# The FFN's down product of a decoder block by one level of Strassen's algorithm, with its input's quarter sums passed through DRAM

## The chip, the cores and the metric

One NeuronCore of a Trainium2 chip runs the whole kernel. The metric is device time in microseconds of one execution; each number quoted for a kernel is the median of its timed runs, and one further execution was recorded by the hardware profiler. All matrix products are made in three passes: an fp32 operand x is split into h (x rounded to the engine's fp32r type) and l = x - h, and x·w is summed as xl·wh + xh·wh + xh·wl. Every product below therefore needs three matmuls where one would stand.

## The reference, cut to what matters

The block is a gated token mixer followed by a SwiGLU FFN, for 512 tokens of width 2048 and a hidden width of 5632:

```python
h2 = rms_norm(x, g_pre_ffn[l]) * (1 + scale_f) + shift_f
f = (jax.nn.silu(h2 @ w_ffn_gate[l]) * (h2 @ w_ffn_up[l])) @ w_ffn_down[l]
x = x + gate_f * rms_norm(f, g_post_ffn[l])
```

The last product, (512 x 5632) @ (5632 x 2048), is the down product. The norm behind it needs the sum of squares of a token's whole row of f, so no output can be finished before all of that token's row is there.

## The kernel before

**The plan.** The kernel is one list `plan` of `Step`s. A step has a source in DRAM (`src`, up to 128x1024 of weights), the matmuls that use it (`mm`), and optional hooks. `run` walks the list and writes the instructions of all engines, each engine then works its own queue in that order. At step i it first emits the `post` hook of step i-1 and the `pre` of step i; then, for the steps up to i+`ahead` (2, or 3 in the Strassen steps), it loads (`fetch`, a DMA on SP's queue into one of the rotating `raw` tiles) and divides (`divide`, line 80's helpers: ACT casts `raw` to `wh`, DVE subtracts to get `wl`); then loads up to i+`far`; then the `late` hook of step i-1; then the matmuls of step i. `fix` is a hook that adds weight tiles together on DVE before they are divided (`prefix`, called two steps further ahead). So what stands in a `post` hook comes on its engine before the split of step i+`ahead`, what stands in a `late` hook comes behind it.

**The up product.** It already goes by one level of Strassen's algorithm (Winograd's form): `strassen(u)` for each of the units 1 to 10 of 512 hidden columns (unit 0 is done plainly by `fill`). Both operands are cut in halves of tokens (HT = 256), inner dimension and columns; seven products of quarter size take the place of eight. Eight pairs of steps (`mm1` for PSUM banks A and B, `mm2` for D and C) are followed by four blocks of three steps (`mm3_` for A, `mm4` for D, `mm5` for C); the sums of weights are made by `fix1` (a 1024-wide and a 512-wide add; the second is also written to DRAM as `t2_d` by POOL's queue) and `fix5`. At the seam between pairs and blocks the hooks `post1`, `late1`, `post2`, `late2` move banks through `u2` and `hn`. The result `hn` (tokens x 512 hidden) of unit u-1 is turned by `hid_out` during unit u: 16 PE transposes into bank B, ACT copies to `hT`, POOL's queue writes four 256 KB tiles `hid_d`.

**The down product.** Two halves g of 1024 output columns, each over 44 steps k of 128 hidden rows. A step loads a 128x1024 weight tile, reads back `hid_d[k]` (POOL's queue, `h_load`), splits both (`divide`, `d_split`), and runs 24 matmuls `d_mm` (four token tiles, two column tiles, three passes) into eight banks. `down_first` starts with half the banks because the last unit's transposes still need the others. In the last four steps of the second half the order is turned to go token tile by token tile, so that `d_evac`, `d_sum` and `d_end` of the tiles 0 to 2 (squares on ACT, scaling, root, four adds with `x1` and the stores) run beside the matmuls of the next tile. `x1` is read back by POOL's queue in the steps 26 to 29 of the second half, four loads of 256 KB each.

Of the kernel before, what the change touches and what calls it, by code (L numbers as in the profile page):

```python
# [15 lines left out]
P = 128  # L16
S = 512
# [16 lines left out]
LAST = 4  # L34
# [40 lines left out]
def body(ctx, tc, nc, a, out):  # L75
# [81 lines left out]
    more = {"F": 1 << 30}  # L157

    def fetch(i):
        o = i - more["F"] - 4  # L160
        if o >= 0 and o % 6 < 3:
# [38 lines left out]
    def divide(i):  # L200
        if i < len(plan) and i not in parts:
            while i not in loaded:
                load(i)
            st, raw = plan[i], loaded[i]
            prefix(i)
            o = i - more["F"] - 2
            p, n = (more["p"], 2) if o >= 0 and o % 5 < 2 else (wp, 3)
            h = p.tile([P, 1024], F32R, name="wh", tag="wh", bufs=n)
# [1104 lines left out]
    hid = {}  # L1313
    hid_d = [drp.tile([P, S], F32, name=f"hid_d{k}") for k in range(KF)]
    t2_d = [[drp.tile([P, 1024], F32, name=f"t2_d{i}{m}") for m in range(4)] for i in range(2)]
# [62 lines left out]

    def hid_out(u, js, bs):

        for j, b in zip(js, bs):
            for t in range(4):
                nc.tensor.transpose(b[:, t * P:(t + 1) * P], hn_of(u, t)[:, j * P:(j + 1) * P], ident)
# [15 lines left out]
    def strassen(u):  # L1399
# [51 lines left out]
        for m in range(4):  # L1451
# [28 lines left out]
            def mm5(h, l, m=m):  # L1480
                for j in range(2):
                    product(B["C"], Xh[:, 1, 8:], Xl[:, 1, 8:], 2 * m + j, h, l, j, False, m == 3 and j == 1)
                if m < 2:
                    hid_out(u - 1, range(2 * m, 2 * m + 2), B["B"])
# [11 lines left out]
            plan.append(Step(src5, mm5, fix=fix5, post=post5 if end else None, late=late5 if end else None, **kw))  # L1496
# [8 lines left out]

    def d_start():
        O["sp"].release()
        xpool.release()
        p = E["p"] = pool("dp")
        E["row"] = p.tile([P, D], F32, name="frow")  # L1510
        gq.dma_start(E["row"], gg_d[16:32].rearrange("a b -> (a b)").partition_broadcast(P))
        E["f"] = p.tile([P, 4, 1024], F32, name="fo")
        E["ssq"] = p.tile([P, 4, 4], F32, name="fssq")
        E["sum"] = p.tile([P, 8], F32, name="fsum")
        E["pad"] = p.tile([P, 104], F32, name="fpad")

    def h_load(k):
        p, tag, n = (E["p"], "hin", 4) if "p" in E else (O["xp"], "hT", 3)
        hid[k] = p.tile([P, S], F32, name=tag, tag=tag, bufs=n)
        gq.dma_start(hid[k], hid_d[k])  # L1520

    def d_split(k):
        p, n = (E["p"], LAST) if "p" in E else (O["xp"], 1)
        hh = p.tile([P, S], F32R, name="hh", tag="hh", bufs=n)
        hl = p.tile([P, S], F32R, name="hl", tag="hl", bufs=n)
        split(hid.pop(k), hh, hl)
        E[k] = hh, hl

    def d_open():
        for k in range(3):  # L1530
            h_load(k)
        d_split(0)

    plan[-1].pre = d_open

    def d_tiles():
        E["g1"] = E["p"].tile([P, 4, 1024], F32, name="fo1")
        E["x1"] = E["p"].tile([P, 4, D], F32, name="x1")

    def f_of(t, g, c):  # L1540
        return E["f" if g == 0 else "g1"][:, t, c * 512:(c + 1) * 512]

    def x1_of(t, c):
        return E["x1"][:, t, c * 512:(c + 1) * 512]

    def d_square(t, g, c):
        junk = E["p"].tile([P, 512], F32, name="junk", tag="junk", bufs=2)
        act(junk, E["ps"][t, c], AF.Square, accum_out=E["ssq"][:, t, g * 2 + c:g * 2 + c + 1])

    def d_scale(t, g, c):  # L1550
        o = g * 1024 + c * 512
        tt(f_of(t, g, c), E["ps"][t, c], E["row"][:, o:o + 512], ALU.mult)

    def d_evac(t, g, c):
        d_square(t, g, c)
        d_scale(t, g, c)

    def d_mm(t, c, k, h, l):
        hh, hl = E[k]
        nat3(E["ps"][t, c], hh[:, t * P:(t + 1) * P], hl[:, t * P:(t + 1) * P], h[:, c * 512:(c + 1) * 512],  # L1560
             l[:, c * 512:(c + 1) * 512], k == 0, k == KF - 1)

    def d_add(t, c, r):

        f, o = f_of(t, c // 2, c % 2), c * 512
        stt(f, f, r, x1_of(t, c), ALU.mult, ALU.add)
        sy.dma_start(out[t][:, o:o + 512], f)

    def d_end(t):

        d_square(t, 1, 1)
        r = E["p"].tile([P, 1], F32, name="rd", tag="rd", bufs=4)
        act(r, E["ssq"][:, t, 3:4], AF.Sqrt, bias=E["sum"][:, t:t + 1], scale=1.0 / D)
        for late in E.pop("late", ()):
            d_add(*late)
        inv(r)
        for c in range(3):
            d_add(t, c, r)
        d_scale(t, 1, 1)
        if t == 3:  # L1580
            d_add(t, 3, r)
        E["late"] = [(t, 3, r)]

    def d_sum(t):
        s = E["sum"][:, t:t + 1]
        nc.vector.reduce_sum(out=s, in_=E["ssq"][:, t, 0:3], axis=AX.X)
        ts(s, s, 1.0 / D, ALU.mult, EPS, ALU.add)

    def down_first(h, l, k):

        E["w", k] = h, l
        if k == 0:
            E["ps"] = {(t, 0): ps_mm("dn") for t in range(4)}
        for t in range(4):
            d_mm(t, 0, k, h, l)
        if k == 0:
            hid_out(UNITS - 1, range(4), [ps_aux("ht") for _ in range(4)])
        if k == 2:
            E["ps"].update({(t, 1): ps_aux("dn") for t in range(4)})
            for kk in range(3):  # L1600
                for t in range(4):
                    d_mm(t, 1, kk, *E["w", kk])

    for g in range(2):
        for k in range(KF):
            def mm(h, l, g=g, k=k):
                if g == 0 and k < 3:
                    down_first(h, l, k)
                    return
                if k == 0:  # L1610
                    b = banks("dn")
                    E["ps"] = {(t, c): b[t * 2 + c] for t in range(4) for c in range(2)}
                if g == 0 or k < KF - LAST:
                    for t in range(4):
# [60 lines left out]
def layout(inp):  # L1675
# [26 lines left out]
    o["w_ffn_down"] = g["w_ffn_down"][0].reshape(KF, P, 2, 1024).transpose(2, 0, 1, 3)  # L1702
# [33 lines left out]
```

## Time and profile before

| | us |
|---|---|
| median of 3 runs (2649.78 to 2652.05) | 2650.61 |
| the profiled execution, own time | 2651.23 |
| its span, first to last instruction | 2649.3 |

| engine | busy us | share of the span |
|---|---|---|
| PE (TensorE) | 2604.2 | 98% |
| DVE (VectorE) | 1707.3 | 64% |
| ACT (ScalarE) | 1048.1 | 40% |
| POOL (GpSimd) | 245.7 | 9% |

The up product's Strassen units run from about 1369 to 2159 us, the down product from 2159 to the end. The rows further down give each engine's queue as the profiler saw it; an operation's duration is longer than the distance between two starts when operations overlap in the pipeline, so both are read: the mean duration from the groups, the distance from the timeline. Sizes are KB of 1024 bytes, rates GB/s of 10^9 bytes.

### The profile page before, as it was taken

The numbers are of one execution on the slowest core, as the hardware profiler recorded it, in microseconds if no ns is written. First come the engines' busy times: TensorE is split into PE (matmuls) and PEld (weight loads), VectorE is DVE, ScalarE is ACT, GpSimd is POOL, SyncE is SP. The second block draws the span as 40 slices with busy tenths as digits, with TensorE's granted clock in tenths as the row PEclk, the third lists the DMA queues.
The fourth block names the chain that finished last, engine by engine and source line by source line (L and its number), as shares of the span: only waits on it lengthen the run. The fifth ranks groups of instructions, "written<-read, shape, count | busy, mean of one in ns | idle before, by whom it ended". The sixth has DMA issues, their size and how long they took to land.

```text
span 2649.3 us, 31866 instructions
## 1 busy us (share of the span) xinstructions
PE 2604.2 (98%) x11757; PEld 2148.7 (81%) x11757; DVE 1707.3 (64%) x2397; ACT 1048.1 (40%) x1428; POOL 245.7 (9%) x454
## 2 busy tenths in 40 slices
PE   6999999999999999999999999999999999999998
PEld 4888888888888888888878888888888888888887
DVE  8888653568547777556687777777777753334334
ACT  4432244442432222447654444444444442223222
POOL 0000002110002111000000000000000011000020
PEclk9999999999999999999999999999999999999999
DMA  9886536433328887567656666655665664454462
GB/s 347 322 293 231 168 96 201 137 127 122 114 92 302 290 289 247 179 197 243 216 190 206 206 192 206 212 195 192 209 199 195 214 235 143 144 147 148 145 207 96
DMA packets 168653, 522.71 MB, mean 197 GB/s; under 512 B 20161, under 2 KB 20177, under 8 KB 167601
## 3 DMA queue, kind: packets, MB, share of 16 engines
q1 hardware_dynamic: 124866, 376.20, 43.0%
q0 software_dynamic: 43632, 144.49, 16.1%
q8 instruction: 92, 1.51, 0.2%
q14 instruction: 63, 0.52, 0.1%
HBM read 468.16 MB, written 52.45 MB: 197 GB/s over the span
## 4 chain that ended last, share of the span: by engine, by line
PE 90%; DVE 4%; ACT 3%; issue 2%; DMA 1%; SPq 0%; DVEq 0%; ACTq 0%
PE st L1396 25%; PE ps L261 7%; PE ps L263 7%; PE ps L262 7%; PE dn L266 6%; PE dn L268 6%; PE dn L267 6%; PE po L266 2%; PE po L267 2%; PE po L268 2%; ACT wh L96 1%; DVE wl L80 1%; PE ups L261 1%; PE w_v L266 1%; PE w_v L267 1%
## 5 line engine op out<-in xcount | busy, mean ns | idle before, releaser
L80 DVE TENSOR_TENSOR wl<-wraw,wh 128x1024 fp32r<-128x1024 f32 (+1 forms) x459 | 557.9, 1222 | 436.7 <-ACT wh L96 426.1
L96 ACT CAST wh<-wraw 128x1024 fp32r<-128x1024 f32 (+1 forms) x459 | 478.8, 1049 | 573.1 <-PE ps L263 202.3
L80 DVE TENSOR_TENSOR wl<-xraw,wh 128x1024 fp32r<-128x1024 f32 x183 | 221.6, 1222 | 101.9 <-ACT wh L96 101.6
L266 PE MATMUL dn<-wh,hl 128*128 128x512 f32 x704 | 274.0, 389 | 0.0
L268 PE MATMUL dn<-wl,hh 128*128 128x512 f32 x704 | 273.9, 389 | 0.0
L267 PE MATMUL dn<-wh,hh 128*128 128x512 f32 x704 | 273.9, 389 | 0.0
L1396 PE MATMUL st<-wh,Xl 128*128 128x512 f32 x640 | 252.5, 394 | 7.8 <-DVE st L80 4.3
L1396 PE MATMUL st<-wl,Xh 128*128 128x512 f32 x640 | 249.8, 390 | 1.8 <-DVE wl L80 1.8
L1396 PE MATMUL st<-wh,Xh 128*128 128x512 f32 x640 | 249.8, 390 | 0.0
L96 ACT CAST wh<-xraw 128x1024 fp32r<-128x1024 f32 x183 | 190.4, 1052 | 115.9 <-PE st L1396 96.8
L87 DVE SCALAR_TENSOR_TENSOR modw<-modw,cb 128x1024 f32<-128x1024 f32 x192 | 228.4, 1220 | 6.0 <-DMA modw<-in_w_mod_dram 6.0
L80 DVE TENSOR_TENSOR hl<-hin,hh 128x512 fp32r<-128x512 f32 x85 | 58.8, 692 | 265.5 <-ACT hh L96 262.3
L261 PE MATMUL ps<-Xh,wl 128*128 128x512 f32 x576 | 228.9, 397 | 0.0
L263 PE MATMUL ps<-Xl,wh 128*128 128x512 f32 x576 | 224.4, 390 | 0.0
L262 PE MATMUL ps<-Xh,wh 128*128 128x512 f32 x576 | 224.2, 389 | 0.0
L96 ACT CAST hh<-hin 128x512 fp32r<-128x512 f32 x85 | 53.0, 624 | 306.8 <-PE dn L268 306.8
L268 PEld LDWEIGHTS dn<-wl,hh 128*128 128x128 f32 x704 | 132.1, 188 | 27.6
L266 PEld LDWEIGHTS dn<-wh,hl 128*128 128x128 f32 x704 | 132.1, 188 | 27.4
L267 PEld LDWEIGHTS dn<-wh,hh 128*128 128x128 f32 x704 | 132.1, 188 | 27.3
L1396 PEld LDWEIGHTS st<-wh,Xl 128*128 128x128 f32 x640 | 120.4, 188 | 36.8 <-DVE st L80 8.5
L1396 PEld LDWEIGHTS st<-wl,Xh 128*128 128x128 f32 x640 | 120.4, 188 | 27.4 <-DVE wl L80 2.2
L1396 PEld LDWEIGHTS st<-wh,Xh 128*128 128x128 f32 x640 | 120.5, 188 | 23.7
(332 smaller groups left out, 4907.6 us busy)
## 6 DMA issues: line engine op xcount, KB each, us to landing
modw<-in_w_mod_dram SPq DMA_DIRECT2D x100, 512.0 KB, 6.4
modw<-in_w_mod_dram POOLq DMA_DIRECT2D x92, 512.0 KB, 5.6
xraw<-in_w_gu_dram SPq DMA_DIRECT2D x92, 512.0 KB, 4.2
wraw<-in_w_gu_dram SPq DMA_DIRECT2D x68, 512.0 KB, 4.1
wraw<-in_w_out_dram SPq DMA_DIRECT2D x64, 512.0 KB, 3.4
wraw<-in_w_gu_dram SPq DMA_DIRECT2D x118, 256.0 KB, 3.2
xraw<-in_w_ffn_down_dram SPq DMA_DIRECT2D x45, 512.0 KB, 4.1
wraw<-in_w_ffn_down_dram SPq DMA_DIRECT2D x43, 512.0 KB, 4.0
```

The lines of the kernel that those rows point to most:

```text
L80: nc.vector.tensor_tensor(out=o, in0=x, in1=y, op=op)
L87: nc.vector.scalar_tensor_tensor(out=o, in0=x, scalar=s, in1=y, op0=op0, op1=op1, **kw)
L96: nc.scalar.copy(h, src)
L261: nc.tensor.matmul(ps, wl, xh, start=first, stop=False)
L262: nc.tensor.matmul(ps, wh, xh, start=False, stop=False)
L263: nc.tensor.matmul(ps, wh, xl, start=False, stop=last)
L266: nc.tensor.matmul(ps, xl, wh, start=first, stop=False)
L267: nc.tensor.matmul(ps, xh, wh, start=False, stop=False)
L268: nc.tensor.matmul(ps, xh, wl, start=False, stop=last)
L1396: nc.tensor.matmul(bank[t], tok(x, k, t), w[:, ws], start=st, stop=last and w is l, skip_group_check=True)
```

## The change

The down product goes by the same algorithm as the up product. Each half v of 1024 output columns is one run of `down(v)`: 22 pairs of inner tiles p, in each a step `srca` that loads the input sums for the pair and has no matmuls, and steps `mm1` and `mm2`; then 11 blocks m with two steps `srcb` of 768 columns that load the other sums and have no matmuls, and `mm3_`, `mm4`, `mm5`. `quarter` makes one quarter product of an inner tile: two token tiles, three passes, six matmuls. The sums of the input's quarters are not made there but once, where the hidden tiles are turned: `hid_out` transposes tiles i and i+2 of a unit into two banks, and `hid_sums`, a `late` hook in the up product's steps m = 0 and 1, makes four quarters `sa` and three `sb` with two ACT copies and four 256-wide DVE operations; POOL's queue writes them to `sa_d` (512 KB) and `sb_d` (384 KB). For the last unit the turning happens in `mm2` of p = 0, and bank B's and C's products of p = 0 and 1 are made behind it, in `mm2` of p = 1. `raw` tiles rotate over nine buffers (three new, `draw`), `wh` and `wl` over eight (three new). The order by token tile in the last steps goes, and `LAST` with it; `x1` is loaded by sixteen loads in one `late` hook of the second block of v = 1.

```diff
-            o = O["xp"].tile([P, S], F32, name="hT", tag="hT", bufs=3)
-            nc.scalar.copy(o, b)
-            gq.dma_start(hid_d[u * 4 + j], o)
...
+            def late6(m=m):
+                hid_sums(u - 1, m, B["B"])
...
+    def hid_sums(u, i, bs):
+        p = O["xp"]
+        sa = p.tile([P, 4, HT], F32, name="sa", tag="sa", bufs=2)
+        sb = p.tile([P, 3, HT], F32, name="sb", tag="sb", bufs=1)
+        nc.scalar.copy(sb[:, 0:2, :], two(bs[1]))
+        nc.scalar.copy(sa[:, 0, :], bs[0][:, :HT])
+        tt(sa[:, 2, :], sb[:, 1, :], bs[0][:, HT:], ALU.subtract)
+        tt(sa[:, 3, :], sa[:, 0, :], bs[0][:, HT:], ALU.subtract)
+        stt(sa[:, 1, :], sa[:, 2, :], -1.0, sa[:, 0, :], ALU.mult, ALU.subtract)
+        stt(sb[:, 2, :], sa[:, 1, :], -1.0, sb[:, 0, :], ALU.mult, ALU.subtract)
+        gq.dma_start(sa_d[u * 2 + i], sa)
+        gq.dma_start(sb_d[u * 2 + i], sb)
...
+    def d_end(t, c, x, s):
+        d_square(t, c, x)
         r = E["p"].tile([P, 1], F32, name="rd", tag="rd", bufs=4)
+        act(r, E["ssq"][:, t, c:c + 1], AF.Sqrt, bias=E["sum"][:, t:t + 1], scale=1.0 / D)
+        d_scale(t, c, x, s)
         inv(r)
+        for i in range(4):
+            d_add(t, i, r)
...
+    def quarter(bank, x, i, h, l, c, first, last):
+        xh, xl = x
+        ws = slice(c * 512, c * 512 + 512)
+        for t in range(2):
+            xs_ = slice(i * HT + t * P, i * HT + t * P + P)
+            for n, (y, w) in enumerate(((xl, h), (xh, h), (xh, l))):
+                nc.tensor.matmul(bank[t], y[:, xs_], w[:, ws], start=first and n == 0, stop=last and n == 2,
+                                 skip_group_check=True)
...
+    def down(v):
+        kw = dict(dur=2.7, ahead=3, far=6)
...
+            def mm1(h, l, p=p):
+                quarter(B["A"], E["a", p], 0, h, l, 0, p == 0, p == NP - 1)
+                if v == 0 and p < 2:
+                    E["x", p] = h, l
+                else:
+                    quarter(B["B"], E["a", p], 1, h, l, 1, p == 0, p == NP - 1)
...
+            def mm2(h, l, p=p):
+                quarter(B["D"], E["a", p], 2, h, l, 0, p == 0, p == NP - 1)
+                if v == 0 and p == 0:
+                    E["z"] = h, l
+                    hid_out(UNITS - 1, 0, B["B"])
+                    hid_out(UNITS - 1, 1, B["C"])
                     return
+                if v == 0 and p == 1:
+                    for q, (zh, zl) in enumerate((E["z"], (h, l))):
+                        quarter(B["B"], E["a", q], 1, *E["x", q], 1, q == 0, False)
+                        quarter(B["C"], E["a", q], 3, zh, zl, 1, q == 0, False)
                     return
+                quarter(B["C"], E["a", p], 3, h, l, 1, p == 0, p == NP - 1)
...
+            plan.append(Step(srca, keep, pre=d_start if v == p == 0 else None, **{**kw, "dur": 0.0}))
+            plan.append(Step(src1, mm1, fix=fix1, post=post1 if end else None, late=late1 if end else None, **kw))
+            plan.append(Step(src2, mm2, post=post2 if end else hid_last if v == p == 0 else None,
+                             late=late2 if end else None, **({**kw, "ahead": 2} if v == 0 and p == 1 else kw)))
...
+            def late_v22():
+                for t in range(2):
+                    d_square(2 + t, 2 + v, O["hn1"][t])
+                    d_scale(2 + t, 2 + v, O["hn1"][t], -1.0)
+                for t in range(4 if v else 0):
                     for c in range(4):
+                        gq.dma_start(E["x1"][:, t, c * 512:(c + 1) * 512], x1_d[t][:, c * 512:(c + 1) * 512])
...
+                plan.append(Step(srcb, keep, n=3 * HT, **{**kw, "dur": 0.0}))
+            plan.append(Step(lambda raw, pair=pair: pair(raw, 1, 0), mm3_, late=late_a if end else None, **kw))
+            plan.append(Step(lambda raw, pair=pair: pair(raw, 0, 1), mm4, late=late_d if end else None, **kw))
+            plan.append(Step(src5, mm5, fix=fix5, post=post_c if end else None, late=late_v22 if m == 1 else None, **kw))
```

`src1`, `fix1`, `src2`, `pair`, `src5`, `fix5` and the hooks `post1` to `late2` are as in the up product. `late_a`, `late_d` and `post_c` take the finished banks A, D and C: a square on ACT and a scaling on DVE for each of two token tiles; in v = 1, `late_a` also makes the sums of squares so far, and `late_d` and `post_c` call `d_end` for the token tiles 0, 1 and 2, 3.

## Rows read from the trace of the kernel before

**Rows 1.** The page's busy part: busy us (share of the span) and instructions.
```profile
PE 2604.2 (98%) x11757; PEld 2148.7 (81%) x11757; DVE 1707.3 (64%) x2397; ACT 1048.1 (40%) x1428; POOL 245.7 (9%) x454
```

**Rows 2.** Windows: stretch, its length, busy us of engines; clock, DMA share, GB/s.
```profile
core 0: us, PE busy (x) PEld busy (x) DVE busy (x) ACT busy (x) POOL busy (x), PEclk, DMA share, GB/s
1454.00:1532.00 78.00, 77.57 (x350) 64.08 (x349) 58.58 (x61) 34.51 (x40) 6.45 (x12) 1.00 0.62 200
2156.00:2400.00 244.00, 243.54 (x1082) 201.50 (x1082) 91.03 (x99) 76.01 (x105) 27.89 (x52) 1.00 0.51 157
0.00:66.00 66.00, 42.28 (x133) 29.69 (x134) 52.92 (x98) 26.83 (x40) 0.69 (x6) 0.92 0.93 347
...
2540.00:2560.00 20.00, 20.00 (x90) 16.55 (x89) 6.31 (x7) 5.24 (x7) 7.83 (x15) 1.00 0.96 327
```

**Rows 3.** Timeline of PE, the down product's first and last matmul: start, duration, instruction.
```profile
2159.46 0.39 PE L266 MATMUL dn<-wh,hl 128*128 128x512 f32 x1
...
2640.66 0.39 PE L268 MATMUL dn<-wl,hh 128*128 128x512 f32 x1
```

**Rows 4.** Groups from 1285 us on: count | busy us, mean ns | idle before.
```profile
L266 PE MATMUL dn<-wh,hl 128*128 128x512 f32 x704 | 274.0, 389 | 0.0
L1383 PE MATMUL ht<-ident,hn 128*128 128x128 f32 x16 | 2.3, 279 | 0.5 <-DVE hn L87 0.5
L80 DVE TENSOR_TENSOR Xl<-h2f,Xh 128x256 fp32r<-128x256 f32 x16 | 6.8, 424 | 4.8 <-ACT Xh L1267 4.8
```

**Rows 5.** Timeline of DVE in an up unit; in brackets the wait before.
```profile
1812.49 1.23 DVE L80 TENSOR_TENSOR wl<-wraw,wh 128x1024 fp32r<-128x1024 f32 x1 [0.51 <-ACT wh L96]
...
1848.83 1.22 DVE L80 TENSOR_TENSOR wraw<-xraw,wraw 128x1024 f32<-128x1024 f32 x1
1850.08 0.69 DVE L80 TENSOR_TENSOR xraw<-wraw,xraw 128x512 f32<-128x512 f32 x1
1850.69 2.35 DVE L80 TENSOR_TENSOR wl<-xraw,wh 128x1024 fp32r<-128x1024 f32 x2
1852.96 1.95 DVE L80 TENSOR_TENSOR wraw<-wraw 128x1024 f32<-128x1024 f32 x2
```

**Rows 6.** Timeline of ACT around the start of the down product.
```profile
2156.17 1.05 ACT L96 CAST wh<-xraw 128x1024 fp32r<-128x1024 f32 x1
2158.98 1.28 ACT L90 ACTIVATE u<-st 128x512 f32<-128x512 f32 x2 [1.76 <-PE st L1396]
```

**Rows 7.** Waits of PE from 1454 to 2156: us in total, times, longest.
```profile
PE st L1396 <- DVE st L80: 3.9, 9, 0.4
```

**Rows 8.** Timeline of DVE in the tail.
```profile
2642.33 2.08 DVE L87 SCALAR_TENSOR_TENSOR fo<-fo,rd,x 128x512 f32<-128x512 f32 x3
2644.32 0.68 DVE L80 TENSOR_TENSOR fo<-dn,frow 128x512 f32<-128x512 f32 x1
2645.04 0.75 DVE L87 SCALAR_TENSOR_TENSOR fo<-fo,rd,x 128x512 f32<-128x512 f32 x1
```

**Rows 9.** DMA issues from 2440 to 2530, then 2539 to 2558: KB, us to landing.
```profile
xraw<-in_w_ffn_down_dram SPq DMA_DIRECT2D x9, 512.0 KB, 4.1
...
x<-x_d POOLq DMA_DIRECT2D x12, 256.0 KB, 7.8
xraw<-in_w_ffn_down_dram SPq DMA_DIRECT2D x3, 512.0 KB, 8.1
```

**Rows 10.** Timeline of PE at two waits; windows of the clock after each.
```profile
1368.95 0.79 PE L1396 MATMUL st<-wh,Xl 128*128 128x512 f32 x1 [3.50 <-ACT hn L90]
1378.38 0.50 PE L1396 MATMUL st<-wl,Xh 128*128 128x512 f32 x1 [1.76 <-DVE wl L80]
...
1366.00:1370.00 4.00, 1.05 (x3) 0.86 (x4) 4.00 (x4) 3.38 (x5) 0.00 (x0) 0.84 0.22 66
1370.00:1374.00 4.00, 4.00 (x15) 3.18 (x14) 3.44 (x5) 0.45 (x1) 0.23 (x1) 0.73 0.66 187
1378.00:1382.00 4.00, 3.62 (x16) 3.00 (x17) 3.97 (x5) 1.86 (x3) 0.72 (x2) 1.00 0.71 246
```

More of the change, by code (lines that the diff above doesn't have):

```diff
@@ L33 @@
 MODS_M = 18
-LAST = 4
 EV_SLACK = 0.0
@@ L155, in body @@
     prepared = {"n": 0, "f": 0.0}
-    more = {"F": 1 << 30}
+    more = {"F": 1 << 30, "G": 1 << 30}
     def fetch(i):
-        o = i - more["F"] - 4
-        if o >= 0 and o % 6 < 3:
+        o, g = i - more["F"] - 4, i - more["G"] - 6
+        if g >= 0:
+            o = (more["G"] + 2 - more["F"] + g // 9 * 6 + g % 9 - 3) if g % 9 >= 3 else -1
+        if g >= 0 and g % 9 < 3:
+            raw = more["d"].tile([P, 1024], F32, name="draw", tag="draw", bufs=3)
+        elif o >= 0 and o % 6 < 3:
             raw = more["p"].tile([P, 1024], F32, name="xraw", tag="xraw", bufs=3)
@@ L205, in divide @@
             prefix(i)
-            o = i - more["F"] - 2
+            o, g = i - more["F"] - 2, i - more["G"] - 3
+            if g >= 0:
+                o = more["G"] + 1 - more["F"] + g // 8 * 5 + g % 8 - 3
             p, n = (more["p"], 2) if o >= 0 and o % 5 < 2 else (wp, 3)
+            if g >= 0 and g % 8 < 3:
+                p, n = more["d"], 3
             h = p.tile([P, 1024], F32R, name="wh", tag="wh", bufs=n)
@@ L1307, in body @@
                                  post=(lambda hf=hf, g=g: mix_done(hf, g)) if k == KD - 1 else None))
-    hid = {}
-    hid_d = [drp.tile([P, S], F32, name=f"hid_d{k}") for k in range(KF)]
-    t2_d = [[drp.tile([P, 1024], F32, name=f"t2_d{i}{m}") for m in range(4)] for i in range(2)]
+    sa_d = [drp.tile([P, 4, HT], F32, name=f"sa_d{p}") for p in range(KF // 2)]
+    sb_d = [drp.tile([P, 3, HT], F32, name=f"sb_d{p}") for p in range(KF // 2)]
+    t2_d = [[drp.tile([P, 1024], F32, name=f"t2_d{i}{m}") for m in range(KF // 4)] for i in range(2)]
     B = {}
@@ L1483, in mm5 @@
                 if m < 2:
-                    hid_out(u - 1, range(2 * m, 2 * m + 2), B["B"])
+                    hid_out(u - 1, m, B["B"])
             def post5():
@@ L1495, in strassen @@
             plan.append(Step(lambda raw, pair=pair: pair(raw, 0, 1), mm4, late=post4 if end else None, **kw))
-            plan.append(Step(src5, mm5, fix=fix5, post=post5 if end else None, late=late5 if end else None, **kw))
+            def late6(m=m):
+                hid_sums(u - 1, m, B["B"])
+            plan.append(Step(src5, mm5, fix=fix5, post=post5 if end else None,
+                             late=late5 if end else late6 if m < 2 else None, **kw))
     fill(0)
@@ L1503, in body, with hid_out @@
         strassen(un)
+    def hid_out(u, i, bs):
+        for j, b in zip((i, i + 2), bs):
+            for t in range(4):
+                nc.tensor.transpose(b[:, t * P:(t + 1) * P], hn_of(u, t)[:, j * P:(j + 1) * P], ident)
+    def hid_sums(u, i, bs):
[10 more added lines that the diff above has]
+        gq.dma_start(sb_d[u * 2 + i], sb)
     def d_start():
@@ L1509, in d_start @@
         p = E["p"] = pool("dp")
+        more["d"] = p
+        for n in ("wh", "wl"):
+            p.tile([P, 1024], F32R, name=n, tag=n, bufs=3)
         E["row"] = p.tile([P, D], F32, name="frow")
         gq.dma_start(E["row"], gg_d[16:32].rearrange("a b -> (a b)").partition_broadcast(P))
-        E["f"] = p.tile([P, 4, 1024], F32, name="fo")
+        E["f"] = p.tile([P, 4, D], F32, name="fo")
+        E["x1"] = p.tile([P, 4, D], F32, name="x1")
         E["ssq"] = p.tile([P, 4, 4], F32, name="fssq")
-        E["sum"] = p.tile([P, 8], F32, name="fsum")
@@ L1515, in d_start @@
[L1515 to L1548, printed above, removed]
@@ L1569, in d_end, with f_of, d_square, d_scale @@
-    def d_end(t):
-        d_square(t, 1, 1)
+        E["sum"] = p.tile([P, 4], F32, name="fsum")
+        nc.vector.memset(E["ssq"], 0.0)
+    def f_of(t, c):
+        return E["f"][:, t, c * 512:(c + 1) * 512]
+    def d_square(t, c, x):
+        junk = E["p"].tile([P, 512], F32, name="junk", tag="junk", bufs=1)
+        act(junk, x, AF.Square, accum_out=E["ssq"][:, t, c:c + 1])
+    def d_scale(t, c, x, s):
+        stt(f_of(t, c), x, s, E["row"][:, c * 512:(c + 1) * 512], ALU.mult, ALU.mult)
@@ L1572, in d_end @@
+    def d_add(t, c, r):
+        f = f_of(t, c)
+        stt(f, f, r, E["x1"][:, t, c * 512:(c + 1) * 512], ALU.mult, ALU.add)
+        sy.dma_start(out[t][:, c * 512:(c + 1) * 512], f)
+    def d_end(t, c, x, s):
+        d_square(t, c, x)
         r = E["p"].tile([P, 1], F32, name="rd", tag="rd", bufs=4)
-        act(r, E["ssq"][:, t, 3:4], AF.Sqrt, bias=E["sum"][:, t:t + 1], scale=1.0 / D)
-        for late in E.pop("late", ()):
-            d_add(*late)
+        act(r, E["ssq"][:, t, c:c + 1], AF.Sqrt, bias=E["sum"][:, t:t + 1], scale=1.0 / D)
+        d_scale(t, c, x, s)
@@ L1576, in d_end @@
         inv(r)
[L1577 to L1582, printed above, removed]
+        for i in range(4):
+            d_add(t, i, r)
     def d_sum(t):
         s = E["sum"][:, t:t + 1]
-        nc.vector.reduce_sum(out=s, in_=E["ssq"][:, t, 0:3], axis=AX.X)
+        nc.vector.reduce_sum(out=s, in_=E["ssq"][:, t, :], axis=AX.X)
         ts(s, s, 1.0 / D, ALU.mult, EPS, ALU.add)
[L1589 to L1602, printed above, removed]
@@ L1651, in body @@
+    more["G"] = len(plan)
+    for v in range(2):
+        down(v)
     begin()
```

145 lines of the change are left out of this document (87 added, 58 removed).

## The prediction

> **What bounds the kernel now.** I read the page first: PE is busy 98% of the span, DVE 64% [rows 1]. That mean hides stages, so the windows come next. One unit of the up product (78 us) has PE busy 77.6 us at full clock, DVE 58.6 us, and the DMA engines 62% busy at 200 GB/s [rows 2]; the down product's stretch 2156 to 2400 has PE busy 243.5 of 244 us, with DVE at 91.0 and DMA at 51%. So in the down product TensorE alone sets the time and all else has room; an edit there is worth its matmuls until another engine fills up. The first and last matmul of the down product start at 2159.46 and 2640.66 [rows 3]. Between them lie 3 x 704 = 2112 matmuls [rows 4] and 16 transposes, so a matmul costs (481.2 - 2.4) / 2112 = 0.2267 us of PE (its 389 ns in the group is latency; starts are 0.227 apart). 2.4 us is the transposes' and their 0.5 us wait. The tail from the last matmul's end (2641.05) to the end of the span (2649.3) is 8.25 us.
>
> **Matmuls removed.** Per half v the change runs seven quarter products over 22 pairs of tiles, six matmuls each: 2 x 22 x 7 x 6 = 1848. It removes 264, and 264 x 0.2267 = **-59.8 us**. The transposes stay 16 per unit.
>
> **VectorE in the pair stretch, the first place to look.** Each pair p now has three splits (`srca`, `src1`, `src2`) and `fix1` (1024 and 512 wide) for 24 matmuls = 5.44 us of PE. The 1222 ns of a split is not its rate: back to back, two splits and then the next start take 2.27 us, 1.135 each; the 1024-wide add and its dependent 512-wide one take 1.25 + 0.61 [rows 5]. So 3 x 1.135 + 1.86 = 5.27 us: DVE is at 97% of PE and still under it. Term: 0. Lower bound 0, as PE is the floor; upper bound from the busy durations without overlap, 3 x 1.222 + 1.219 + 0.692 = 5.58, 0.14 over PE, x 44 = 6 us. I take 0, since the rows run at the pitch for whole chains. What it does cost is spare time: only 0.17 us per pair is won back, so a delay at a seam is not quickly made up.
>
> **The block stretch (two `srcb`, `mm3_`, `mm4`, `mm5`).** 36 matmuls = 8.16 us. DVE: three splits and `fix5` at 1.135, two 768-wide splits at about 0.87 (between the 512 and 1024 pitches) = 6.3 us. But eight `wh`/`wl` buffers in rotation put the split of the next `mm4` on a buffer that `mm5` still reads: cast 1.05 [rows 6] plus split 1.22 plus semaphores is 2.35 us after `mm5`'s end, against 2.72 us of `mm3_` as cover. The other five follow by 7.5 of 8.16 us. Term 0, with 0.4 us of slack.
>
> **Up to down seam.** T is the end of the last `st` matmul. Silu ends at T+0.63 (ACT starts it before T, [rows 6]); the cast for the second pair's `srca` follows it, and DVE makes that split before `late5`, so `hn` is whole at T+4.1. PE has 12 matmuls (2.72 us) until the transposes, which need `hn`: 1.4 us idle. Then `fix1` stands ahead of the split of `src2` of the second pair, done at T+8.25 where PE is ready at 7.05: 1.2 us. `hid_sums` for the last unit (four 256-wide operations, some 0.42 us each [rows 4], twice) comes behind that split and is done with bank B before PE wants it at T+9.65. Before, PE lost 0.5 us there. Term **+2.5** (0 to 7).
>
> **Pair to block seam, twice.** In the up product this seam costs 0.4 us per unit [rows 7], because three steps with matmuls are ready. Here two of the three prepared steps are `srcb`, with none. From T, the end of the last `mm2`: `hn1` by T+1.3 on DVE, bank D copied on ACT by 1.95, then cast 3.0, split of `mm4` at 4.25 against 2.72: 1.5 us. `late2` runs four 0.6 us operations and the split of `mm5` ends at 7.85 against 6.97: 0.9. The two `srcb` splits, `fix5` and the next `mm3_` end at 11.95 against 10.6: 1.35. `late_v22` later pushes one more `mm3_` by 0.9. **+4.7 each, 9.4** (0 to 16; zero if DVE were free there, 16 if its lead at T is nil and `late1` adds 1.2 and jitter as much again).
>
> **Half to half seam.** At the end of v=0 DVE has six evictions of 0.65 us, `fix1` twice and splits in line: bank A free 0.95 us late, bank D 0.95, the `mm1` after next 1.5 and 0.25. **+3.7** (0 to 6).
>
> **Tail.** Before, the last token tile alone ended behind the last matmul. After, `mm4`'s bank gives two `d_end` and `mm5`'s two more; each is a scale, an inverse and four adds. The adds pitch at 0.665 (2.08 for three [rows 8]), so a `d_end` is 0.62 + 0.2 + 2.66 = 3.5 us. The first can start adding at T-0.8, after square, table load and root; the fourth ends at T+12.4. From the last add to the end it was 2649.3 - 2645.8 = 3.5 us. So 15.9 against 8.25: **+7.7** (5 to 11).
>
> **Transfers.** A pair moves 512 (`sa`) + 512 + 256 KB in and 256 KB out per 5.44 us, a block 2 x 384 + 3 x 512 KB per 8.16 us: both 289 GB/s. Rows 2 give 200 GB/s at 62% (323 if full), 327 at 96% (341), 347 at 93% (373). So the stream needs 77 to 89% of the engines. Nine `raw` buffers let a load start nine steps ahead, 14.7 us, while loads land in 4.1 us [rows 9]. Term 0. The sixteen loads of `x1` (4.19 MB) are another matter: before they went out at 96 GB/s of weights; now they come at once in the second half's block stretch. By the spare 341 - 289 = 52 GB/s over the 73 us left, 3.8 of 4.19 MB are absorbed. If they took half the engines, weights would get 170 GB/s for 24.6 us, 10.1 us of stream short, of which 14.7 - 8.1 (the slowed landing in rows 9) - 3.3 (`fix5` comes two steps early) = 3.3 us is covered: 6.8. Term **+3** (0 to 10).
> The Trainium skill, DMA: Bandwidth & Descriptors, section on queues, rings and completion order, says that a DMA engine takes turns between the queues that have work, a packet at a time; by it alone the half share, and +6.8 in place of +3, would hold. The row of before shows weight loads landing in 8.1 instead of 4.1 us beside `x1`, which agrees in direction.
>
> **Up units.** `hid_sums` puts four 256-wide operations behind the transposes of steps m=0 and m=1, on DVE behind the split of the step three ahead. They are done 2.7 us after the transposes; the next split is due 10.9 us after, bank B again after 8.2 us, and DVE has 19 of 78 us free [rows 2]. What is queued behind them is `fix5` and the next splits; nobody waits. On POOL two writes of 512 and 384 KB replace two pairs of 256 KB. Term 0 (0 to 5 over ten units).
>
> **Sum.** -59.8 + 2.5 + 9.4 + 3.7 + 7.7 + 3 = -33.5. The profiled execution took 2651.23 us (span 2649.3 and 1.9 outside); its median of three is 0.6 lower. 2650.6 - 33.5 = **2617**.
>
> **Rivals.** (1) Slower: DVE meets ACT at each split. Where lookahead fails, DVE waits 0.51 us for the cast [rows 5]; with three such waits a pair costs 5.27 + 1.53 = 6.8 us, 1.36 over PE, x 44 = 60: **2677**. It decides from 0.32 us per split, (0.17 + 33.5 / 44) / 3. For it: DVE at 97%. Against: eight buffers, so ACT, with 3.15 us of casts in 5.44, runs ahead. (2) TensorE's clock falls at the new seams. After an idle stretch of 3.50 us the granted clock was 0.84 and 0.73 of full in the next two 4 us windows, that is 3.4 us at the lower of its levels (1.2 against 2.4 GHz) and 1.7 us lost; after one of 1.76 us it stayed 1.00 [rows 10]. If each of some eleven new waits did so, +19: **2636**. My waits are 1.5 us or less, so it should not.
> The Trainium skill, TensorE: Matmul & The Clock Gate, section on HAM oscillation, tells of a loop that falls to half rate at each wait for data; the trace has that for the long wait and not for the short one.
> (3) The DMA engines fill up, the stream lagging over the whole block stretch besides `x1`: at 275 GB/s for the two block stretches (180 us x 289/275) +9, and `x1` at 6.8 in place of 3: **2630**. (4) The seams hide, as DVE enters them with more lead than I give: 15.6 us less: **2601**. (5) The change doesn't do what it says: the saving is eaten elsewhere in the down product, **2650**.
>
> **How the numbers follow.** Forecast 0.70, 2617, its own range 2606 to 2629. Rival 1: 0.04; 2: 0.07; 3: 0.08; 4: 0.08; 5: 0.03. The range leaves out rivals 1 and 5 and takes in the others and the bounds: 2600 to 2638. Faster by over 0.2% (5.3 us, about what a measurement of this kernel can tell) has all of the forecast and of rivals 2 to 4: 0.93; same 0.03; slower 0.04.
>
> **What would show it.** In the profile after: 1848 down matmuls at 0.227 us apart; DVE almost without gaps in the pair stretches, at 5.44 us per pair (at 6 or more rival 1 is right); PE waits for `wl` of 1 to 2 us grouped at the three kinds of seam, some 15 us in all; granted clock 1.00 in them; 15 to 16 us from the last matmul to the end; DMA at 75 to 90% and, beside `x1`, near 100%. Gaps of PE spread evenly over the pairs, or a wait for loads outside the `x1` window, would make the prediction wrong.

## The result and the profile after

The changed kernel takes 2620.93 us (median of four runs, 2617.24 to 2622.03), the kernel before 2651.33 beside it: a ratio of 0.9881 with a 95% interval of 0.9864 to 0.9898, some 30 us less. The forecast was 2617 in a range of 2600 to 2638. The profiled execution has a span of 2619.7 us, 29.6 under the 2649.3 of before.

The page's busy part, then the busy tenths of the DMA engines in 40 equal slices of the span:

```profile
PE 2552.8 (97%) x11493; PEld 2101.9 (80%) x11493; DVE 1951.1 (74%) x2678; ACT 1142.6 (44%) x1502; POOL 222.3 (8%) x410
DMA  9886536442327888366746666666666668888896
```

11757 matmuls in [rows 1] have become 11493, 264 fewer. DVE rises from 64% to 74%. Of its 244 us more, 213 lie in the last sixth of the span, the down product, where the DMA engines now stand at 8 tenths; the rest is ahead of it, where `hid_sums` was added. The windows of the down product show the stages (columns as in [rows 2]):

```profile
2162.00:2166.00 4.00, 3.21 (x18) 2.28 (x17) 4.00 (x7) 2.84 (x4) 0.22 (x1) 1.00 1.02 290
2166.00:2170.00 4.00, 2.94 (x19) 2.27 (x16) 0.55 (x1) 0.86 (x2) 0.00 (x0) 1.00 1.02 406
2170.00:2174.00 4.00, 0.00 (x0) 0.00 (x0) 2.59 (x3) 0.00 (x0) 0.38 (x1) 1.00 1.02 410
2174.00:2178.00 4.00, 3.48 (x9) 2.78 (x10) 1.89 (x5) 0.00 (x0) 1.23 (x3) 0.58 0.92 359
2178.00:2182.00 4.00, 0.40 (x2) 0.00 (x0) 0.81 (x3) 1.70 (x4) 0.00 (x0) 0.85 0.35 144
2182.00:2186.00 4.00, 3.91 (x9) 3.14 (x10) 3.97 (x5) 2.97 (x4) 1.07 (x2) 0.50 0.52 174
2186.00:2190.00 4.00, 4.00 (x15) 3.20 (x14) 3.97 (x5) 3.06 (x4) 0.54 (x1) 0.80 0.94 368
2190.00:2290.00 100.00, 100.00 (x443) 82.80 (x442) 96.62 (x93) 55.23 (x55) 9.72 (x18) 1.00 0.89 293
2290.00:2320.00 30.00, 27.92 (x119) 21.80 (x118) 25.23 (x30) 18.12 (x24) 0.00 (x0) 1.00 0.72 236
2320.00:2390.00 70.00, 70.00 (x310) 57.97 (x309) 57.25 (x55) 39.25 (x49) 0.54 (x1) 1.00 0.86 292
2390.00:2500.00 110.00, 110.00 (x487) 91.06 (x486) 109.32 (x107) 62.73 (x67) 12.54 (x24) 1.00 0.87 286
2500.00:2530.00 30.00, 27.91 (x119) 21.81 (x118) 24.13 (x27) 15.74 (x20) 7.34 (x14) 1.00 1.02 397
2530.00:2600.00 70.00, 70.00 (x310) 57.96 (x310) 56.52 (x57) 39.64 (x49) 0.00 (x0) 1.00 0.71 241
```

In the long stretches PE is busy without a gap: 100 of 100 us beside a DVE at 96.6, 110 of 110 beside one at 109.3, 70 of 70 twice. What is lost is lost at seams, and by far the most at the first one, 2162 to 2190, where the granted clock falls to its lower level (0.50 from 2182 to 2186). PE's waits from 2140 us on, in total, and then each from the timeline:

```profile
PE st L1583 <- DVE wl L79: 9.6, 7, 5.6
PE st L1583 <- DVE sa L79: 3.7, 1, 3.7
PE st L1514 <- DVE hn L86: 0.8, 2, 0.5
...
2174.52 0.79 PE L1583 MATMUL st<-wl,wh 128*128 128x512 f32 x1 [5.58 <-DVE wl L79]
2182.09 0.76 PE L1583 MATMUL st<-wh,wl 128*128 128x512 f32 x1 [3.69 <-DVE sa L79]
2301.89 0.50 PE L1583 MATMUL st<-wl,wh 128*128 128x512 f32 x1 [0.53 <-DVE wl L79]
2305.42 0.50 PE L1583 MATMUL st<-wl,wh 128*128 128x512 f32 x1 [0.50 <-DVE wl L79]
2309.42 0.50 PE L1583 MATMUL st<-wl,wh 128*128 128x512 f32 x1 [0.97 <-DVE wl L79]
```

The same three waits (0.53, 0.50, 0.98) stand in the second half, at 2514 to 2523. The down product's first matmul starts at 2161.22 and its last ends at 2603.66: 442.4 us, against 481.6 between the same points before. The tail is 16.0 us, against 8.25. The 1.8 us that are missing to 29.6 lie ahead of the down product, whose start varies by 3 us even between kernels that are alike up to there (the same transposes of hidden tiles stand at 2132.6 in e4 and 2135.6 in e9, two of the kernels below).

### The profile page after: what moved, and what is told of

It reads as the page before. It is cut to its first block, busy times and chain, and to the rows that moved or that the text cites. A ratio compares the mean times of both kernels' runs of the same rounds, so it can differ in the third digit from the quotient of the medians.

```text
span 2619.7 us, 32219 instructions
## 1 busy us (share of the span) xinstructions
PE 2552.8 (97%) x11493; PEld 2101.9 (80%) x11493; DVE 1951.1 (74%) x2678; ACT 1142.6 (44%) x1502; POOL 222.3 (8%) x410
## 3 DMA queue, kind: packets, MB, share of 16 engines
q0 software_dynamic: 41520, 141.60, 15.3%
## 5 line engine op out<-in xcount | busy, mean ns | idle before, releaser
L79 DVE TENSOR_TENSOR wl<-wraw,wh 128x1024 fp32r<-128x1024 f32 (+2 forms) x497 | 597.1, 1212 | 410.9 <-ACT wh L95 400.0
L95 ACT CAST wh<-wraw 128x1024 fp32r<-128x1024 f32 (+2 forms) x497 | 513.0, 1042 | 654.9 <-PE ps L271 202.2
L79 DVE TENSOR_TENSOR wl<-xraw,wh 128x1024 fp32r<-128x1024 f32 (+1 forms) x219 | 259.3, 1204 | 77.2 <-ACT wh L95 76.6
L95 ACT CAST wh<-xraw 128x1024 fp32r<-128x1024 f32 (+1 forms) x219 | 223.6, 1039 | 185.8 <-PE st L1395 101.0
L1583 PE MATMUL st<-wl,wh 128*128 128x512 f32 x616 | 242.1, 393 | 9.6 <-DVE wl L79 9.6
L1583 PE MATMUL st<-wh,wl 128*128 128x512 f32 x616 | 241.7, 392 | 3.8 <-DVE sa L79 3.7
L1583 PE MATMUL st<-wh 128*128 128x512 f32 x616 | 241.2, 391 | 0.0
L1583 PEld LDWEIGHTS st<-wl,wh 128*128 128x128 f32 x616 | 116.5, 189 | 37.0 <-DVE wl L79 12.6
L1583 PEld LDWEIGHTS st<-wh,wl 128*128 128x128 f32 x616 | 116.7, 189 | 28.9 <-ACT sa L1522 4.1
L1583 PEld LDWEIGHTS st<-wh 128*128 128x128 f32 x616 | 116.6, 189 | 24.4
```

The costliest lines, as they stand in the source:

```text
L79: nc.vector.tensor_tensor(out=o, in0=x, in1=y, op=op)
L95: nc.scalar.copy(h, src)
L1583: nc.tensor.matmul(bank[t], y[:, xs_], w[:, ws], start=first and n == 0, stop=last and n == 2, skip_group_check=True)
```

## The experiments

Two questions were open. Why is the first seam 10 us of waits, where 2.5 were forecast? And are the claims right that held, DVE's spare 0.17 us per pair and the tail being DVE's queue? All times below are medians with the ratio to the kernel before (near 2652 us in each of three sets: e1 to e4, e5 to e8, e9 and e10). Only the second set has the changed kernel beside it, so a difference of less than some 4 us from it is inside the intervals of the ratios; what such an edit did is read from the waits.

**The changed kernel again** (e8), as the base on the chip of the second set:

> The changed kernel itself, on the same chip as the runs beside it, so that they are compared with it and not only with the kernel before. 2618 to 2622, 30 to 32 us under the kernel before.

2620.86 us, ratio 0.9883 (0.987 to 0.9897). The two long waits at the first seam are 6.2 and 3.2 us in this execution, against 5.6 and 3.7: such a wait differs by half a microsecond with nothing changed.

**A tile of its own for the last `sb`** (e1). The second of the last unit's two `hid_sums` shares the one `sb` buffer with the first.

```diff
+        if u == UNITS - 1 and i == 1:
+            sb = E["f"][:, 3, :3 * HT].rearrange("p (a t) -> p a t", a=3)
+        else:
+            sb = p.tile([P, 3, HT], F32, name="sb", tag="sb", bufs=1)
```

> One edit to the changed kernel: the last unit's second sb tile gets memory of its own (a piece of fo, unused then), so that its ACT copy no longer waits for the first sb's write to DRAM. My theory: PE's second wait at the up-to-down seam (3.69 us before a matmul into bank C) is that wait; it goes, and with it the stretch at the lower clock behind it (13 matmuls, some 2.6 us): 5 to 6.5 us faster than the changed kernel, about 2615. Rival, bank C is late because DVE was late (fix1 and the loads before it): no gain, 2621, and the wait only changes its releaser.

2614.29 us, ratio 0.9858 (0.9844 to 0.9873): 6.6 faster than the changed kernel. In the changed kernel's timeline of ACT and DVE the wait can be read, and in e1's that it is gone:

```profile
2180.30 0.59 ACT L1521 COPY sb<-st 128x512 f32<-128x512 f32 x1 [13.12 <-DMA sb_d<-sb]
2181.19 0.42 DVE L79 TENSOR_TENSOR sa<-sb,st 128x256 f32<-128x256 f32 x1 [5.27 <-ACT sa L1522]
```
```profile
2164.78 0.59 ACT L1524 COPY sb<-st 128x512 f32<-128x512 f32 x1 [1.48 <-issue]
...
2165.61 0.59 ACT L1524 COPY fo<-st 128x512 f32<-128x512 f32 x1
```

ACT stood 13.12 us until the first `sb` was in DRAM, in front of every cast behind it, and bank C was free only then. Not all of it is the store: DVE finished the first `hid_sums`, behind `fix1`, only at 2175.9, the store was issued at 2176.5 and took 3.7 us. In e1 no wait for bank C is left, and the lower clock behind it (13 matmuls at 0.43 instead of 0.227 us apart, 2.7 us) went with it; the first wait stays, 5.3 us. So PE's wait of 3.69 us is that buffer. My theory holds, the rival falls.

**`frow` later** (e2). The 1 MB broadcast load of `frow` moves from the seam to pair 8.

```diff
-        gq.dma_start(E["row"], gg_d[16:32].rearrange("a b -> (a b)").partition_broadcast(P))
+            def row_in():
+                gq.dma_start(E["row"], gg_d[16:32].rearrange("a b -> (a b)").partition_broadcast(P))
...
+                             late=late1 if end else row_in if v == 0 and p == 8 else None, **kw))
```

> One edit to the changed kernel: the 1 MB broadcast load of frow goes out in the late hook of pair 8 of the first half, not at the seam. If PE's first wait at the seam (5.58 us) is set by the crowd of loads that start at one moment (some 4.7 MB at 407 GB/s), a megabyte less brings fix1 about 2.6 us forward and the time to about 2618.5. Rival, POOL's queue doesn't share engines with SP's loads in that stretch: the second draw load still lands 9 us after its issue, no gain.

2618.0 us, ratio 0.987 (0.9854 to 0.9887): 2.9 faster, which the times alone do not show, but the first wait fell from 5.58 to 3.13 us, by about the 2.6 of my theory, while the second was 4.19. So the loads share the engines. In the changed kernel eight loads on SP's queue and `frow` were issued from 2161.4 to 2166.9. The new `draw` tiles lie in space that the up product held: SP's queue waited 8.9 us for its matmuls before the first `draw` load, and five more loads stood in the queue behind the three. The third `draw` load, the 256 KB of `src2`, took 9.0 us to land (issues 2160 to 2176):

```profile
frow<-gg_d POOLq DMA_DIRECT2D x1, 1024.0 KB, 9.4
draw<-sa_d SPq DMA_DIRECT2D x1, 512.0 KB, 4.5
draw<-in_w_dn_dram SPq DMA_DIRECT2D x1, 512.0 KB, 5.9
...
draw<-in_w_dn_dram SPq DMA_DIRECT2D x1, 256.0 KB, 9.0
```

**`fix1` of the third pair behind the work that is due** (e3).

```diff
-                if st.far:
+                if st.far and (j + 2 != more["G"] + 7 or i > more["G"] + 3):
                     prefix(j + 2)
```

> One edit to the changed kernel: fix1 of the third pair is emitted two steps later, so that on DVE it stands behind the split of the second pair's src2 and behind hid_sums, not ahead of them. My theory: PE's 5.58 us wait is DVE standing in fix1 for a load that the next matmuls don't need; it goes with its stretch at the lower clock (7 matmuls, 1.4 us): up to 7 us faster. But the wait on bank C (sb's write) then comes sooner and is some 3 to 5 us itself, so 2614 to 2617 in all. Rival, the load is needed at once anyway: the wait moves to the third pair's mm1 at the same size, 2621.

2619.02 us, ratio 0.9876 (0.9861 to 0.9891): 1.9 faster than the changed kernel, too little for these times to show and less than my theory gave (4 to 7). The first wait went, as the theory had it, but the second grew from 3.69 to 9.42 us: ACT's second `sb` copy still waited 11.66 us for the first one's store. I had put the store at 3 to 5 us. Issued at 2170.0 and not at 2176.5, it went out into the crowd of loads (DMA share 1.02 and 1.03 from 2170 to 2178) and took 9.0 us in place of 3.7, and PE stood there.

**Both edits, `sb` and `fix1`** (e4).

> Both edits, e1 and e3. My theory: both waits and both stretches of lower clock go, 12 to 14 us faster than the changed kernel, 2607 to 2609, with no wait of PE over 1 us left in the down product. Rival (a third wait stands behind them, a load or DVE's backlog at 97%): 2612 to 2616, with a wait for wl at the third or fourth pair.

2609.03 us, ratio 0.9838 (0.9823 to 0.9853): 11.9 faster than the changed kernel. All that is left of PE's waits from 2140 us on is this, and the window 2160 to 2200 has the full clock:

```profile
PE st L1586 <- DVE wl L79: 5.2, 9, 1.0
PE st L1514 <- DVE hn L86: 0.8, 2, 0.5
...
2160.00:2200.00 40.00, 37.95 (x171) 30.06 (x170) 37.10 (x44) 21.49 (x25) 5.38 (x10) 1.00 0.97 353
```

Apart the two gave 6.6 and 1.9, together 11.9: the waits stand one behind the other on PE, and with the first alone gone PE stood longer in the second. No wait is over 1 us, as the theory said, and the gain is at the lower end of what it gave.

**The three together** (e7).

> The two edits of e4 with that of e2 (frow's load later). With fix1 behind the needed splits no matmul waits for the crowded loads any more, so e2's 2.9 us should be gone: within 1 us of e4, 2608 to 2609. Rival, the small waits left behind the seam in e4 (0.30, 0.47, 0.49 us) are the loads: up to 1.5 us faster.

2608.57 us, ratio 0.9837 (0.9823 to 0.985): the same as e4. With `fix1` in its new place the crowd of loads costs nothing that the times can show. In the trace two of e4's three small waits behind the seam are gone (0.26 us is left of 1.26), so they were the loads, as the rival has it; but the third wait at the second pair-to-block seam is 1.71 and not 0.99, for a load beside `x1` (see below).

**A dose for DVE** (e5). One 512-wide add per pair, from the fifth pair on.

```diff
                 tt(raw[:, 512:], z[:, :512], raw[:, 512:], ALU.add)
+                if 4 <= p:
+                    tt(E["p"].tile([P, 512], F32, name="junk", tag="junk", bufs=1), raw[:, :512], raw[:, 512:], ALU.add)
```

> One DVE operation more per pair, from the fifth pair of each half on: a 512-wide add of fp32 into a scratch tile nobody reads, 0.6 us back to back, 36 of them. My theory: DVE needs 5.27 of the 5.44 us that PE gives a pair, so 0.17 us of the 0.6 are free and 0.43 to 0.5 come through each time: 36 x 0.43 = 15 us and up to 18 slower than the changed kernel, 2635 to 2639, with waits of PE for wl spread over the pairs. Rival, DVE has more room than the pitches say (the wait for ACT's casts is the slack): under 5 us slower. Rival the other way, DVE is the bound already: the full 36 x 0.6 = 22 us, 2643.

2639.73 us, ratio 0.9959 (0.9946 to 0.9971): 18.9 slower than the changed kernel. DVE's timeline of one pair, and the window of the first pair stretch:

```profile
2239.43 1.94 DVE L79 TENSOR_TENSOR xraw<-xraw 128x1024 f32<-128x1024 f32 x2
2241.41 0.69 DVE L79 TENSOR_TENSOR junk<-xraw 128x512 f32<-128x512 f32 x1
2242.02 1.22 DVE L79 TENSOR_TENSOR wl<-draw,wh 128x1024 fp32r<-128x1024 f32 x1
2243.15 2.35 DVE L79 TENSOR_TENSOR wl<-xraw,wh 128x1024 fp32r<-128x1024 f32 x2
2245.42 1.95 DVE L79 TENSOR_TENSOR wraw<-wraw 128x1024 f32<-128x1024 f32 x2
...
2200.00:2290.00 90.00, 87.28 (x372) 68.66 (x372) 88.98 (x92) 44.33 (x46) 8.19 (x16) 1.00 0.80 264
```

From one `fix1` to the next it is 5.99 us, 0.72 more than the 5.27 of the prediction, so the dose costs 0.72 with its dependence. DVE now sets the pair's time, 0.55 us above the 5.44 of PE, which leaves 0.17 us that were free, the prediction's figure. By the times 18.9 / 36 = 0.525 came through, just above my 0.43 to 0.5; the five runs spread from 2637.0 to 2645.6, so this way of reckoning gives 0.2 free only roughly. The changed kernel is not bound by DVE in the pairs, and a fifth of a microsecond more per pair would make it so.

**The tail: two of four adds off DVE** (e6, on top of e4).

```diff
+        if c in (0, 2):
+            act(f, f, AF.Copy, scale=r[:, 0:1])
+            nc.gpsimd.tensor_tensor(out=f, in0=f, in1=xx, op=ALU.add)
+        else:
+            stt(f, f, r, xx, ALU.mult, ALU.add)
```

> The two edits of e4, and in the tail two of the four adds of each d_end leave DVE: ACT multiplies by the root, POOL adds x1. My theory: the 16 us behind the last matmul are DVE's queue of four d_end at 3.45 us; with 1.33 us less in each, the last add ends some 4 to 5 us earlier if POOL's add of 128x512 takes under 1.3 us, 2604 to 2605, against 2609 for e4. Rival: POOL's adds are slower than 2 us each, the tail is POOL's then: same as e4 or slower.

2612.61 us, ratio 0.9853 (0.9839 to 0.9866): 3.6 slower than e4. POOL's adds took 1.5 us each, between the two bounds of the expectation, but DVE's slowed beside them:

```profile
2599.19 2.96 POOL L1563 TENSOR_TENSOR fo<-fo,x 128x512 f32<-128x512 f32 x2 [0.38 <-ACT fo L89]
...
2598.39 2.64 DVE L86 SCALAR_TENSOR_TENSOR fo<-fo,rd,x 128x512 f32<-128x512 f32 x2
```

Two adds in 2.64 us, where they pitched at 0.665 [rows 8]: DVE ran no faster than POOL. So the edit moved work to where it took time from DVE again. From the last matmul to the end it takes 18.3 us, against 16.0 in e4. That the tail is DVE's queue is not shown by this run; it is read from the trace of the changed kernel (below) and from e10.

**One more step divided ahead at the pair-to-block seams** (e9, on top of e7).

```diff
+            kw = dict(dur=2.7, ahead=4 if end else 3, far=6)
...
+            kw = dict(dur=2.7, ahead=4 if m == 0 else 3, far=6)
```

> The three edits of e7, and at the two pair-to-block seams one more step divided ahead (4 in place of 3), so that ACT's casts for mm3_ and mm4 stand before its copies of the banks. My theory: the three waits at each seam (0.53, 0.50, 0.97 us) are an order on ACT, whose cast for mm4 stands behind copies that wait for the last mm2, while DVE idles 3.1 us for the cast before; they go, with the restart of the pipeline after each: 4 to 5 us faster than e7, about 2604. Rival, DVE has no time there at 97%: the same waits come one step later, 2608 as e7.

2608.41 us, ratio 0.9831 (0.9817 to 0.9844): no difference from e7 that can be measured. The waits became fewer and longer, 0.71 and 1.08 in the first half, 0.63 and 1.63 in the second. That is the rival's outcome: moving ACT's casts forward only moves the place. In the first half DVE still waits 1.64 us for a cast and then works without a gap up to the longer wait, so it has not the time there; of the 1.63 us in the second half 0.46 are DVE's wait for a load beside `x1`.

**One wide add in place of four** (e10, on top of e9).

```diff
-        for i in range(4):
-            d_add(t, i, r)
+        for i in range(0, 4, 2 if t == 3 else 4):
+            o = slice(i * 512, (i + (2 if t == 3 else 4)) * 512)
+            stt(E["f"][:, t, o], E["f"][:, t, o], r, E["x1"][:, t, o], ALU.mult, ALU.add)
+            sy.dma_start(out[t][:, o], E["f"][:, t, o])
```

> e9, and the four 512-wide adds of a d_end become one of 2048 (two of 1024 for the last token tile), each with one store. My theory: the tail is DVE's time for four d_end; the fixed part of three of four operations goes, some 0.13 us each, so 1 to 1.5 us of 16. Against it: the stores start later and the last is larger. Rival: the end is the stores', no gain or up to 1.5 us slower than e9.

2607.85 us, ratio 0.983 (0.9817 to 0.9844): within 0.6 us of e9, which the times cannot tell from none. The trace shows both sides of the expectation:

```profile
2592.71 2.35 DVE L86 SCALAR_TENSOR_TENSOR fo<-fo,rd,x 128x2048 f32<-128x2048 f32 x1
...
2595.77 2.35 DVE L86 SCALAR_TENSOR_TENSOR fo<-fo,rd,x 128x2048 f32<-128x2048 f32 x1
```

A `d_end` takes DVE 3.06 us in place of 3.45, and its last add ends 10.9 us behind the last matmul in place of 12.3 in e9. The end comes 15.3 us behind it in place of 16.1: of the 1.4 us won on DVE, 0.6 go to the last store, which is 512 KB and not 256. e4, e7, e9 and e10 all beat both kernels, by some 12 us the changed one.

## Why the prediction was right, and which of its steps were not

Term by term, from the trace of the changed kernel:

| term | forecast us | measured us |
|---|---|---|
| matmuls | -59.8 | -59.8 (264 fewer, still 0.227 apart) |
| up to down seam | +2.5 (0 to 7) | +14.2 |
| pair to block seams | +9.4 | +4.0 |
| half to half seam | +3.7 | 0 |
| tail | +7.7 | +7.8 |
| `x1` among the loads | +3 | 0 (0.6 in e8) |

The table's last five make 26.0 against 26.3 forecast, so the total came right by luck: one seam was 11.7 us too low, outside its own range of 0 to 7, and three other terms together 12.1 too high. Two of the prediction's own signs of being wrong came, at that seam: a wait for loads outside the `x1` window, and a granted clock below 1.00. Some 4 us more lie in the restart of PE's pipeline after each wait and in the start of the down product (1.8).

**Matmuls and DVE in the pairs: right.** The stretches above have PE at 100% with DVE at 97 to 99%, and the dose shows the margin. Taking the distance between starts [rows 5] and not the duration decided this: by durations a pair would have been 0.14 us over PE. Rival 1 needed 0.32 us of ACT's wait per split; DVE waited for ACT three times from 2190 to 2290 (2.7 us, most of it at the stretch's end) and not once from 2390 to 2500.

**Up to down seam: the step that failed.** The prediction put the third pair's `fix1` ahead of the split of the second pair's `src2` and counted DVE's time for it, not the load that it waits for. Its rows for landing (4.1 us, 8.1 beside `x1`, [rows 9]) were used for the stream and not at the one place where the loads all start together. DVE waited for the third `draw` load, which landed 9.0 us after its issue, with the split that PE needed behind it:

```profile
2165.33 1.22 DVE L79 TENSOR_TENSOR wl<-wraw,wh 128x1024 fp32r<-128x1024 f32 x1
2171.38 1.95 DVE L79 TENSOR_TENSOR draw<-draw 128x1024 f32<-128x1024 f32 x2 [4.83 <-DMA draw<-in_w_dn_dram]
2173.25 1.22 DVE L79 TENSOR_TENSOR wl<-wraw,wh 128x1024 fp32r<-128x1024 f32 x1
```

The second half of the error is bank C: the prediction followed `hid_sums` to bank B and did not ask for how many buffers `sb` has. e1, e3 and e4 show both. The 14.2 are 0.8 + 5.6 + 3.7 of waits and 4.1 of slow clock behind the two long ones (7 and 13 matmuls at 0.43 us).

**The clock, rival 2: half right.** It was priced for eleven short waits, which should not do it and did not: the window with the waits of 0.50 to 0.97 us has 1.00. But the first seam's waits were long, as the one of 3.50 us in [rows 10], and cost the same way: 1.4 and 2.7 us.

**Pair to block seam: a size.** The prediction took bank D as done at the end of the last `mm2`; `mm2` makes D first and C after, so DVE began the sum at 2297.70, with `mm3_` starting at 2298.35, and all that follows came 0.7 to 0.9 us earlier. The order of the three waits is the predicted one. The fourth (0.9, from `late_v22`) did not come. By the matmuls done, the seam costs more than its waits: 119 in the 30 us from 2290 to 2320 are 27.0 us at 0.227, so 3.0 us were lost and 2.0 of them are the listed waits. With the restarts the two seams take 6.0 of the 9.4 forecast.

**Half to half seam: a size.** The prediction had bank A free 0.95 us late. DVE's timeline has it read out by 2388.4, and the next half's `mm1` takes it at 2390.7; banks D and C are read out about a microsecond before they are needed. DVE came to the seam without a wait since 2374.4. Part of that lead can be seen: in the block stretch the prediction let `mm5` hold its `wh` and `wl` buffers to its end, but `mm5` takes the two inputs one after the other, so the first buffer is free 1.36 us sooner, and ACT's casts show that distance:

```profile
2381.42 1.06 ACT L95 CAST wh<-wraw 128x1024 fp32r<-128x1024 f32 x1 [2.75 <-PE st L1583]
2382.78 2.11 ACT L95 CAST wh<-wraw 128x1024 fp32r<-128x1024 f32 x2 [0.30 <-PE st L1583]
```

Whether this is the whole of the lead was not tested.

**`x1` and the DMA engines: the ceiling and the cover were too low.** The stream was put at 77 to 89% and measured 86 to 89 in the three long windows ahead of `x1`. But 341 GB/s, the rate beside `x1` before, is not what the engines can carry: 2500 to 2530 moved 397, 2170 to 2174 moved 410. The half share, the prediction's worse case, did come. From 2500 to 2520, with `x1` under way, POOL's queue (q0, mostly `x1`) and SP's (q1, the stream) show packets, MB and share of 16 engines:

```profile
q0 software_dynamic: 1296, 4.28, 54.1%
q1 hardware_dynamic: 1371, 3.52, 46.1%
```

So the stream got 176 GB/s of its 289 for 20 us and fell 7.8 us behind; in the next 10 us it had nearly all the engines. The Trainium skill, DMA: Bandwidth & Descriptors, section on queues, rings and completion order, says that a DMA engine takes turns between the queues that have work; the trace agrees. What was wrong is the cover, put at 3.3 us: PE's waits there are the seam's, with the sizes of the first half. It was near the edge, though. In e8, the same kernel, DVE waited for a load and PE's third wait was longer by 0.6 us:

```profile
2518.52 1.23 DVE L79 TENSOR_TENSOR draw<-draw,wraw 128x1024 f32<-128x1024 f32 x1 [0.52 <-DMA draw<-t_d]
...
2520.93 0.50 PE L1583 MATMUL st<-wl,wh 128*128 128x512 f32 x1 [1.61 <-DVE wl L79]
```

The Trainium skill, DMA: Bandwidth & Descriptors, section on bandwidth, gives some 425 GB/s for a core that streams alone; the 410 here are near it.

**Tail: right.** DVE's queue of four `d_end`, one after the other, 3.45 us each:

```profile
2602.87 2.74 DVE L86 SCALAR_TENSOR_TENSOR fo<-fo,rd,x 128x512 f32<-128x512 f32 x4
2605.53 0.68 DVE L86 SCALAR_TENSOR_TENSOR fo<-st,frow 128x512 f32<-128x512 f32 x1
...
2606.32 2.74 DVE L86 SCALAR_TENSOR_TENSOR fo<-fo,rd,x 128x512 f32<-128x512 f32 x4
```

Forecast 15.9 from the last matmul to the end, measured 16.0. The 7.8 us are the price of the removed order by token tile, which ran such work beside the matmuls. Of the edits tried only e10 gave some of it back, 0.8 us by its trace.

**Up units: right.** PE waits 4.3 us for bank C (`st`) over ten units before and after, and no wait for `hid_sums` has come.

**Rivals 3 to 5.** Rival 3, a stream that lags over the whole block stretch, did not come: it ran at 292 GB/s in the first half's. Rival 4, seams that hide, came at one of the three kinds of seam, half to half, and in part at pair to block. Rival 5, the saving eaten elsewhere, did not come.

## What to carry to other kernels

Where one pool of tiles takes the place of another, every load into the new tiles starts at one moment; look up what stands in an in-order queue behind the first instruction that needs one of them, and put the work that is due ahead of it. Count the buffers of every tile that is written twice in a row with a store between: one buffer turns a store to DRAM into a wait of the engine that fills it, and the store took 3.7 or 9.0 us here by what else the DMA engines had to do. Take engine rates from the distance between starts, not from durations, and follow a bank's release to the half of the step that finishes it.

## What the runs showed of the hardware that was not expected

DVE's two-input adds from SBUF run at half their rate while POOL adds from SBUF: 1.32 us against 0.665, with POOL at 1.48 (e6). The Trainium skill, SBUF — State Buffer, section Who interferes with whom, says that a DVE instruction with two SBUF inputs contends with a GpSimd instruction that reads SBUF; the trace agrees.

The DMA engines carried 406 to 410 GB/s over 8 us in the crowd at the first seam, against 347 at the most in a window of [rows 2].

A wait of 3.13 us of PE (e2) was followed by a fall of the clock too, but only after six matmuls at about the full rate, where after 3.69 and 5.58 us the first matmul was slow already; the columns are those of PE's timeline:

```profile
2172.07 0.50 PE L1582 MATMUL st<-wl,wh 128*128 128x512 f32 x1 [3.13 <-DVE wl L79]
...
2173.35 0.43 PE L1582 MATMUL st<-wh 128*128 128x512 f32 x1
2173.58 0.63 PE L1582 MATMUL st<-wl,wh 128*128 128x512 f32 x1
2174.01 0.63 PE L1582 MATMUL st<-wh,wl 128*128 128x512 f32 x1
```
